# A hybrid encoder block: the recurrence's lowest levels as one block product, and loads, banks and branch tiles rearranged

## The chip, the core and the metric

The kernel runs on one core of one Trainium2 chip. The metric is device microseconds of one execution. Before the change three runs took 1755.15, 1756.07 and 1757.55 us; the median is 1756.07 us. A separate, profiled execution gave the trace.

## The reference

One layer on x of 1024 tokens by 1024 channels, in float32. An RMS norm and one input projection feed three token mixers and three sigmoid gates of 1024 channels:

- a gated linear recurrence (HGRN2): 4 heads, 128 x 128 state, `S_t = diag(f_t) S_{t-1} + (1 - f_t) i_t^T`, `o_t = S_t^T q_t`, then a norm and a silu gate;
- forgetting attention (FoX): 8 heads of 64, causal, with a bias that is the running sum of log-sigmoid forget values;
- attention into 256 memory tokens, 4 heads of 128.

Each mixer's output is projected to 1024 channels, gated and summed; an output projection and the residual follow. Then come a norm, a feed-forward of width 2816 whose gate branch passes a causal convolution of width 3, and the second residual. The recurrence within a chunk needs `A[t,s] = sum_c q[t,c] k[s,c] exp(G[t,c] - G[s,c])` for s <= t, where G is the running sum of log f.

## The kernel before

Products of float32 precision are made from three fast products: an operand is split into a high part (cast on ScalarE, L115) and the rest (VectorE, L123), and `mm3` (L109 to L111) adds high x high, high x low and low x high. Big projections are cut in quarters and done with seven products instead of eight, from sums and differences of the quarters. These operands are "families" (`B11`, `B21`, `T1` to `T4`, `B22`; tiles of pool `pfam`), split once and kept.

The kernel is written as one stream of instructions through a tile framework. The framework orders each engine's queue ahead of time, with its own model of time; an instruction emitted earlier has a higher priority, and `ahead` (L97) raises the priority of a generator's steps by `AHEAD` = 300 instructions. Within a queue the chip then runs in that fixed order. Tiles with a `tag` and `bufs` are rings: a new tile waits until the oldest of the ring is no longer read. A released pool's space is reused tile by tile.

The stages, in order of time:

1. Memory keys and values (`kv_chunk`), squares and turned rows of x, families. The memory's products stay in four PSUM banks, `pairs[0]` and `pairs[2]` (the two `lg` banks); `pairs` are three pairs out of the eight banks, which the next stages take in turn.
2. Five token-major stages (`stage`, 310 us and before): memory queries, HGRN inputs, two of FoX queries and keys, FoX values. `first_unit` does stage 0 with eight plain products, `tm_unit` the others with seven. Results go to DRAM through `put` functions; a part of a `put` that has to turn rows (`queries`, `keys`, tiles `ko` in a ring of two) is put on `pending` and runs one step later. The list `late` says which side work is emitted after which step of a stage. `memory()` (L405: `mem_norm`, `mem_values`, `mem_keys`) is emitted in stage 0 after its third step; `mem_values` copies the values out of the `lg` banks into `mvf`, a tile of the `ko` ring (L317 to L320). Memory attention (`mem_attn`) is cut into 33 steps on the list `slow`, of which `STAGE_STEPS` = 2 are emitted after each stage step; a value step takes two `tr` banks (L669, L674). `forget_row` (L558) computes the running sum of the forget values in two passes of 512 tokens on 8 partitions.
3. FoX, eight heads (`fox_attn`), woven with the channel-major projections (`cm_unit`: 18 units of 7 steps, 12 matmuls of 512 columns a step) that give the recurrence's inputs and the gates. The generator `fill` yields these steps, and `weave` hands out so many per head (`FOX_FILL`). The mask `mskf` is loaded on SP (L908).
4. The recurrence, four heads by two halves of 512 tokens (`hgrn_mix`), woven with the rest of `fill` (`HGRN_FILL`, with `HGRN_STEPS` = 24 for 18 real steps). A half makes `A` in 128-token blocks: the diagonal and its neighbour by one product with `kt` and `qq` (L1022 to L1037), then six levels of block halves, H = 64, 32, 16, 8, 4, 2 (`LEVELS`): differences of G to a reference (L1050, L1051), one exp (L1052), multiplies on GpSimd and VectorE (L1053, L1054), four plain float32 matmuls (L1063, L1072), and a copy under a mask (L1074). Then state and output, the output's norm, and a turned store (L1115 to L1127).
5. The branches (`branches`, L826): the last 48 steps of `fill`, in the order FoX, memory, recurrence. They are in a pool `gp` of their own, which is opened when the projections' ring pool `ur` and `pfam` are released (L898): the mixer's output `yr` (loaded whole, L833 and L835), its split tiles, weights `braw`, gates `gt` and the sums `mg`.
6. The output projection, and the feed-forward up and down, to 1756 us. Only the release of a pool is changed there.

Of the kernel before, what the change touches and what calls it, by code (L numbers as in the profile page):

```python
# [14 lines left out]
P = 128  # L15
# [14 lines left out]
FOX_STEPS, HGRN_STEPS = 28, 24  # L30
# [3 lines left out]
STAGE_STEPS = 2  # L34
# [33 lines left out]
def tile_block(ctx: ExitStack, tc: tile.TileContext, xT, x_rows, memT, mem_rows, vec, fbias, mats, hmask, w_ff, w_tm, w_cm,  # L68
# [247 lines left out]
    def mem_values():  # L316
        mvf = ko_tile("mvf", F32).rearrange("p a b -> p (a b)")  # L317
        for m in range(2):
            S.activation(mvf[:, m * HB:(m + 1) * HB], pairs[2][m], AF.Copy, scale=rm[:, m:m + 1])
        SP.dma_start(kvd[:, 1, :], mvf)  # L320
# [60 lines left out]
    row_norm(1)  # L381

# [21 lines left out]

    def memory():  # L405
        mem_norm()
        mem_values()
        mem_keys()
# [51 lines left out]
    def tm_unit(u, put, between=None):  # L460

        x, z, y = (pairs[(u + i) % 3] for i in range(3))
# [95 lines left out]
    def forget_row():  # L558
        fb = mem["mp"].tile([8, 2], F32, tag="fb", name="fb")
        SP.dma_start(fb[:, 0:1], fbias)  # L560
        for n in range(2):
            sl = slice(n * HB, (n + 1) * HB)
            a, b = (half_tile(f"fr{i}")[:8, :] for i in range(2))
            SP.dma_start(a, ffd[:, sl])
            V.tensor_scalar(a, a, fb[:, 0:1], None, ALU.add)
            S.activation(b, a, AF.Abs)
            S.activation(b, b, AF.Sigmoid)
            S.activation(b, b, AF.Ln)
            V.scalar_tensor_tensor(out=b, in0=a, scalar=0.0, in1=b, op0=ALU.min, op1=ALU.add)
            V.tensor_tensor_scan(a, ones[:8, :].to_broadcast([8, HB]), b, fb[:, 1:2] if n else 0.0,  # L570
                                 ALU.mult, ALU.subtract)
            SP.dma_start(negFd[:, sl], a)
            if n == 0:
                V.tensor_copy(fb[:, 1:2], a[:, HB - 1:HB])
# [64 lines left out]
    def mem_attn(h, n):  # L639
# [26 lines left out]
        def values(j):  # L666
# [7 lines left out]
            po = ps_tr()[:, 0:256]  # L674
# [28 lines left out]
    stage(0, put_mq, (None, second_half, memory, differences, None, third))  # L703
# [10 lines left out]
    for f in pending:  # L714
        f()
    rp.release()
# [104 lines left out]
    pools, mg, y_last = [], [], []  # L821
# [4 lines left out]
    def branches():  # L826
        gp = tc.alloc_tile_pool(name="gp", bufs=1, side="right", reuse_waits="tile")
        pools.append(gp)
        yr = {}

        def load_y(br):
            yr[br] = gp.tile([P, 4, T], F32, tag="y16", name=f"yr{br}")
            SP.dma_start(yr[br][:, 0:2, :], yd3[br][:, 0:2, :])  # L833
            n = 4 if br else 3
            SP.dma_start(yr[br][:, 2:n, :], yd3[br][:, 2:n, :])  # L835

        load_y(ORDER[0])
        ys = [[gp.tile([P, T], F32R, tag=f"y{p}{k}", name=f"y{p}{k}") for p in "hl"] for k in range(4)]
        yh, yl = [a for a, _ in ys], [b for _, b in ys]

        def chunk(br, j):
            raw = gp.tile([P, HB], F32, tag="braw", name="braw", bufs=2)
            SP.dma_start(raw, w_br[br, j])
            wh, wl = (gp.tile([P, HB], F32R, tag=t, name=t, bufs=3) for t in ("bwh", "bwl"))
            split(S, wh, wl, raw)
# [21 lines left out]
        def load_gates(i):  # L867
            gts[i] = []
            for n in range(2):
                gt = gp.tile([P, HB], F32, tag="gt", name="gt", bufs=3)  # L870
# [3 lines left out]
        for i, (br, j) in enumerate(order):  # L874
            if j == 0:
                for c in range(4 if br else 3):
                    split(S, yh[c], yl[c], yr[br][:, c, :])
# [3 lines left out]
                if i < 16:  # L881
                    load_y(order[i + 8][0])
            load_gates(i)
            if i < 8:
                mg.append(gp.tile([P, T], F32, tag=f"mg{j}", name=f"mg{j}"))
# [8 lines left out]

    def fill_steps():
# [757 lines left out]
```

## Time and profile before

| | |
|---|---|
| median of three runs | 1756.07 us |
| the profiled execution, its own time | 1758.42 us |
| its span, first to last instruction | 1756.6 us |
| mean granted TensorE clock | 0.988 |
| busy share of TensorE, VectorE, ScalarE, GpSimd | 97%, 70%, 48%, 25% |
| DMA traffic | 271.96 MB, mean 155 GB/s |

The profile is a page with busy shares and groups of instructions, and a trace that can be asked: who waited for whom, groups by line and shape, one tile's instructions, windows of time, instructions in order of time. A row of a group gives its line, engine, operation, the tiles (written <- read), the shape and the count, then the busy time, the mean duration in ns, and the idle time of the engine ahead of it with what ended it. Matmuls overlap in the pipeline, so the rate of TensorE is read from one start to the next, not from durations. A plain float32 matmul shows as two records.

### The profile page before, as it was taken

How to read it: one execution, taken by the hardware profiler on the slowest of the kernel's cores; microseconds unless marked ns; L12 is line 12 of the kernel's file. 1: busy time of each engine (PE TensorE's matmuls, PEld its weight loads, DVE VectorE, ACT ScalarE, POOL GpSimd, SP SyncE). 2: the span in 40 equal slices, each digit the busy share in tenths (PEclk: the TensorE clock that was granted, in tenths of full speed). 3: DMA queues.
4: the chain of work that ended last, by engine and by line, in shares of the span. 5: the costliest groups of instructions: out<-in, count | busy, mean ns of one | idle time of the engine just before them, and what ended most of it. 6: DMA issues, size and time to landing. Idle time of an engine off the chain costs nothing.

```text
span 1756.6 us, 25190 instructions
## 1 busy us (share of the span) xinstructions
PE 1706.7 (97%) x9040; PEld 1447.6 (82%) x9040; DVE 1228.1 (70%) x2230; ACT 848.2 (48%) x1463; POOL 440.6 (25%) x471
## 2 busy tenths in 40 slices
PE   7899999899999999898999999999999999999999
PEld 5899999778888888787888888788888888788887
DVE  5764665476766666888987845887777877674654
ACT  8655554365655565756432333643343443433332
POOL 0133533454544443443421000211111111100000
PEclk9999999999999999999999999999999999999999
DMA  7252352754444432524443632565444354494772
GB/s 282 92 181 95 133 208 79 206 160 137 145 144 139 138 104 90 179 91 162 164 154 115 209 133 96 157 174 166 149 133 132 114 156 136 151 361 131 242 266 84
DMA packets 119437, 271.96 MB, mean 155 GB/s; under 512 B 12520, under 2 KB 29544, under 8 KB 118672
## 3 DMA queue, kind: packets, MB, share of 16 engines
q1 hardware_dynamic: 95504, 203.76, 34.9%
q0 software_dynamic: 14592, 51.91, 10.4%
q10 hardware_dynamic: 9216, 14.68, 2.3%
q8 instruction: 71, 1.16, 0.3%
q14 instruction: 54, 0.44, 0.1%
HBM read 202.87 MB, written 90.51 MB: 167 GB/s over the span
## 4 chain that ended last, share of the span: by engine, by line
PE 83%; DMA 5%; DVE 4%; ACT 3%; POOL 2%; issue 1%; SPq 1%; ACTq 0%; DVEq 0%; POOLq 0%
PE pp L109 17%; PE pp L110 17%; PE pp L111 17%; PE lg L109 4%; PE lg L110 4%; PE lg L111 4%; PE tr L109 2%; PE tr L110 2%; PE tr L111 2%; PE lg L1072 1%; PE po L981 1%; DMA gd<-uo 1%; PE lg L939 1%; DMA nf<-negFd 1%; PE lg L940 1%
## 5 line engine op out<-in xcount | busy, mean ns | idle before, releaser
L1331 POOL DMA_DIRECT2D rw<-in_w_up x44 | 24.4, 560 | 358.9 <-DVE wl L123 180.6
L115 ACT CAST wh<-s 128x512 fp32r<-128x512 f32 x85 | 51.9, 619 | 127.0 <-PE pp L110 63.5
L115 ACT CAST dwh<-wr 128x1024 fp32r<-128x1024 f32 (+1 forms) x42 | 41.1, 979 | 126.6 <-PE tr L110 42.6
L115 ACT CAST wh<-rw 128x512 fp32r<-128x512 f32 x65 | 40.0, 619 | 87.3 <-PE pp L110 47.6
L1053 POOL TENSOR_TENSOR X<-X,kt 128x256 f32<-128x256 f32 x48 | 52.1, 1090 | 103.0 <-ACT X L1052 101.5
L123 DVE TENSOR_TENSOR dwl<-wr,dwh 128x1024 fp32r<-128x1024 f32 (+1 forms) x42 | 47.6, 1133 | 41.3 <-ACT dwh L115 41.3
L110 PE MATMUL pp<-yl,bwh 128*128 128x512 f32 x192 | 76.3, 397 | 0.0
L123 DVE TENSOR_TENSOR ul<-us,uh 128x512 fp32r<-128x512 f32 x72 | 54.6, 759 | 30.1 <-ACT uh L115 30.0
L109 PE MATMUL pp<-yh,bwh 128*128 128x512 f32 x192 | 75.6, 397 | 0.0
L111 PE MATMUL pp<-yh,bwl 128*128 128x512 f32 x192 | 75.3, 394 | 0.0
L955 ACT ACTIVATE pt<-pt,st 128x128 f32<-128x128 f32 (+3 forms) x64 | 49.7, 777 | 51.6 <-DVE st L952 26.2
L957 POOL TENSOR_SCALAR pt<-pt,st 128x128 f32<-128x128 f32 (+3 forms) x64 | 53.0, 829 | 44.9 <-DVE st L956 32.4
L115 ACT CAST uh<-us 128x512 fp32r<-128x512 f32 x72 | 44.4, 619 | 38.3 <-PE pp L110 27.0
L123 DVE TENSOR_TENSOR wl<-s,wh 128x512 fp32r<-128x512 f32 x85 | 58.2, 685 | 4.9 <-ACT wh L115 4.9
L726 POOL TENSOR_TENSOR us<-ur 128x512 f32<-128x512 f32 x36 | 46.7, 1297 | 44.9 <-DMA ur<-in_w_cm 27.6
L123 DVE TENSOR_TENSOR wl<-rw,wh 128x512 fp32r<-128x512 f32 x65 | 43.8, 687 | 18.9 <-PE pp L111 12.8
L934 POOL TENSOR_TENSOR nfm<-nf,mskf 128x128 f32<-128x128 f32 x64 | 32.9, 515 | 88.5 <-DVE st L945 51.0
L110 PE MATMUL pp<-dbl,dwh 128*128 128x512 f32 x132 | 52.7, 400 | 1.5 <-DVE dbl L123 1.5
L123 DVE TENSOR_TENSOR ul<-ur,uh 128x512 fp32r<-128x512 f32 x54 | 48.3, 896 | 7.8 <-ACT uh L115 6.8
L726 POOL TENSOR_TENSOR us<-us,ur 128x512 f32<-128x512 f32 x36 | 47.6, 1324 | 24.0 <-DVE ul L123 11.5
L123 DVE TENSOR_TENSOR pl<-tr,ph 128x512 fp32r<-128x512 f32 (+1 forms) x80 | 49.6, 629 | 5.9 <-ACT ph L115 5.8
L111 PE MATMUL pp<-dbh,dwl 128*128 128x512 f32 x132 | 53.0, 402 | 0.0
(623 smaller groups left out, 6288.3 us busy)
## 6 DMA issues: line engine op xcount, KB each, us to landing
rw<-in_w_up POOLq DMA_DIRECT2D x44, 512.0 KB, 4.7
ur<-in_w_cm SPq DMA_DIRECT2D x72, 256.0 KB, 2.9
sd<-in_w_dn POOLq DMA_DIRECT2D x30, 512.0 KB, 5.9
br<-yd SPq DMA_DIRECT2D x30, 512.0 KB, 5.5
gd<-uo ACTq DMA_DIRECT2D x48, 256.0 KB, 2.6
gt<-gd SPq DMA_DIRECT2D x48, 256.0 KB, 2.7
yd<-fc SPq DMA_DIRECT2D x44, 256.0 KB, 2.3
raw<-in_w_tm SPq DMA_DIRECT2D x20, 512.0 KB, 4.3
```

The source lines that it names most:

```text
L109: PE.matmul(ps, lh, rh, start=first, stop=False, skip_group_check=more)
L110: PE.matmul(ps, lh, rl, start=False, stop=False, skip_group_check=more)
L111: PE.matmul(ps, ll, rh, start=False, stop=last, skip_group_check=more)
L115: S.copy(out, in_)
L123: return (sub or V).tensor_sub(l, src, h.bitcast(F32))
L726: G.tensor_add(t, a, b)
L934: G.tensor_tensor(nfm, nf[:, tsl], mskf, ALU.add)
L939: PE.matmul(ps[:, :w], qa[:, tsl], kh[:, s0:s0 + w], start=True, stop=False)
L955: S.activation(pt[:, :ns], pt[:, :ns], AF.Exp, bias=st[:, 2:3], accum_out=st[:, 3:4])
L957: G.tensor_scalar(pt[:, :ns], pt[:, :ns], st[:, 3:4], 0.0, ALU.mult, ALU.add)
L1053: G.tensor_mul(Xk, Xk, Kv[:, :, 0, :])
L1331: late["raw"] = G.dma_start(raw[:, 2 * i:2 * i + 2, :], src[:, 2 * i:2 * i + 2, :])
```

## The change

- **Recurrence.** Only levels 64, 32, 16 and 8 remain. The pair product and the levels 4 and 2 are replaced by one product over blocks of eight tokens: with X = G minus G of the block's fourth token, the operands are k exp(-X) and q exp(X), one matmul per 128 tokens, and one copy under a 512-column mask into `A`. `A` is two fixed tiles that are zeroed once. The mask input shrinks from 7 to 4 parts. `HGRN_STEPS` becomes 14.
- **Output of a half.** Norm, turn and store become `finish`, emitted after the next half's block product; its store one half later.
- **Memory.** `mem_norm` and `mem_values` are emitted ahead of stage 0, `mem_keys` in stage 0 after its fifth step; `mvf` moves to the `e` ring (3 tiles). Three slow steps per stage step; a value step reuses the `tr` bank that it turned into. `forget_row` is one pass on 16 partitions, whose second half gets the first half's last sum by a small transfer.
- **Banks.** Stage 4 takes the pairs turned by one.
- **Loads.** The first two steps of `fill` are emitted ahead of the last `pending` work and of FoX; the load of `mskf` gets a priority of 600 instructions.
- **Branches.** No pool of their own: weights in the ring `ur`, gates in the ring `ue`, the outputs `yr` in families `B11` and `B22`, their splits in `B21` and `T2`, the sums in `T1` and `T3`. The first load of `yr` is emitted after the second step of the last projection unit.

The diff, cut to its core:

```
-FOX_STEPS, HGRN_STEPS = 28, 24
+FOX_STEPS, HGRN_STEPS = 28, 14
...
-STAGE_STEPS = 2
+STAGE_STEPS = 3
...
     def mem_values():
-        mvf = ko_tile("mvf", F32).rearrange("p a b -> p (a b)")
+        mvf = e_tile("mvf").rearrange("p a b -> p (a b)")
...
     row_norm(1)
+    mem_norm()
+    mem_values()
...
-        x, z, y = (pairs[(u + i) % 3] for i in range(3))
+        x, z, y = (pairs[(u + i + (u == 4)) % 3] for i in range(3))
...
     def forget_row():
-        fb = mem["mp"].tile([8, 2], F32, tag="fb", name="fb")
-        SP.dma_start(fb[:, 0:1], fbias)
+        fb = mem["mp"].tile([16, 2], F32, tag="fb", name="fb")
+        V.memset(fb, 0.0)
+        a, b = (half_tile(f"fr{i}")[:16, :] for i in range(2))
         for n in range(2):
...
+        V.tensor_tensor_scan(a, ones[:16, :].to_broadcast([16, HB]), b, 0.0, ALU.mult, ALU.subtract)
+        SP.dma_start(fb[8:16, 1:2], a[0:8, HB - 1:HB])
+        V.tensor_scalar(a, a, fb[:, 1:2], None, ALU.add)
...
-            po = ps_tr()[:, 0:256]
+            po = ptr[:, 0:256]
...
-    stage(0, put_mq, (None, second_half, memory, differences, None, third))
+    stage(0, put_mq, (None, second_half, None, differences, mem_keys, third))
...
     stage(4, put_fqk(1))
-    for f in pending:
-        f()
-    rp.release()
...
     def branches():
-        gp = tc.alloc_tile_pool(name="gp", bufs=1, side="right", reuse_waits="tile")
...
+        halves = [[fam_tile(f, p, (P, 2, T)) for f in ("B21", "T2")] for p in "hl"]
+        yh, yl = ([half[k // 2][:, k % 2, :] for k in range(4)] for half in halves)
...
-            raw = gp.tile([P, HB], F32, tag="braw", name="braw", bufs=2)
+            raw = ur.tile([P, HB], F32, tag="ur", name="ur", bufs=5)
...
+    def load_y(br):
+        yr[br] = [fam_tile(("B11", "B22")[ORDER.index(br) % 2], p, (P, 2, T), F32) for p in "hl"]
...
     def fill_steps():
         for u, spec in enumerate(UNITS):
-            yield from cm_unit(u, [puts_of(*s) for s in spec])
+            for i, _ in enumerate(cm_unit(u, [puts_of(*s) for s in spec])):
+                if u == len(UNITS) - 1 and i == 1:
+                    load_y(ORDER[0])
+                yield
+        yield from branches()
         ur.release()
-        pfam.release()
-        yield from branches()
...
     fill = fill_steps()
+    run_all(islice(fill, 2))
+    for f in pending:
+        f()
+    rp.release()
...
-    SP.dma_start(mskf, mats[:, 2 * P:3 * P])
+    with tc.high_priority(2 * AHEAD):
+        SP.dma_start(mskf, mats[:, 2 * P:3 * P])
...
-    LEVELS = [64, 32, 16, 8, 4, 2]
+    LEVELS = [64, 32, 16, 8]
...
+            A = As[n]
+            X, E = (ph.tile([P, HB], F32, tag="X", name=t, bufs=4) for t in "XE")
+            G8 = Gt.rearrange("p (b e) -> p b e", e=8)
+            V.tensor_sub(X.rearrange("p (b e) -> p b e", e=8), G8, G8[:, :, 3:4].to_broadcast([P, HB // 8, 8]))
+            S.activation(E, X, AF.Exp, scale=-1.0)
+            S.activation(X, X, AF.Exp)
+            G.tensor_mul(E, E, kt)
+            V.tensor_mul(X, X, q)
+            pd = ps_lg()
+            for b in range(4):
+                bs = slice(b * P, (b + 1) * P)
+                PE.matmul(pd[:, bs], E[:, bs], X[:, bs], start=True, stop=True)
+            V.copy_predicated(A, hm[:, 2:4, :].rearrange("p a b -> p (a b)"), pd)
             yield
+            for f in range(len(late)):
+                late.pop(0)()
...
+            late.append(partial(finish, h, n, po, gz))
             yield
```

More of the change, by code (lines that the diff above doesn't have):

```diff
@@ L1 @@
 from contextlib import ExitStack, nullcontext
+from functools import partial
 from itertools import chain, islice
@@ L880, in branches @@
                     split(S, yh[3][:, sl], yl[3][:, sl], t)
-                if i < 16:
-                    load_y(order[i + 8][0])
+                if i == 0:
+                    load_y(ORDER[1])
+            if i == 14:
+                load_y(ORDER[2])
             load_gates(i)
             if i < 8:
-                mg.append(gp.tile([P, T], F32, tag=f"mg{j}", name=f"mg{j}"))
+                if j % 2 == 0:
+                    t = fam_tile(("T1", "T3")[j // 4], "hl"[j // 2 % 2], (P, 2, T), F32)
+                    mg.extend(t[:, i, :] for i in range(2))
             for n, ps in chunk(br, j):
@@ L994, in tile_block @@
     ph = tc.alloc_tile_pool(name="ph", bufs=1, side="left", reuse_waits="tile")
[L995 to L996 removed]
+    hm = ph.tile([P, 4, 256], mybir.dt.uint8, tag="hm", name="hm")
+    hmf = ph.tile([P, 4, 64], F32, tag="X", name="hmf", bufs=4)
     rs = ph.tile([P, HB], F32, tag="rs", name="rs")
@@ L1133, in tile_block @@
         weave((ahead(hgrn_mix(h), AHEAD), HGRN_STEPS), (islice(fill, HGRN_FILL[h]), HGRN_FILL[h]))
+    for f in late:
+        f()
     run_all(fill)
```

124 lines of the change are left out of this document (49 added, 75 removed).

## The prediction

> **What bounds the kernel now.** I read the page first, for the busy shares.
>
> ```profile
> span 1756.6 us, 25190 instructions
> ...
> PE 1706.7 (97%) x9040; PEld 1447.6 (82%) x9040; DVE 1228.1 (70%) x2230; ACT 848.2 (48%) x1463; POOL 440.6 (25%) x471
> ```
>
> TensorE is busy all but 50 us, so only two things can shorten the run: matmul time taken away, and idle or slowed TensorE time taken away. The waits of TensorE say what its idle time waited for (total, times, longest).
>
> ```profile
> PE pp L109 <- DVE ko L123: 5.1, 1, 5.1
> PE lg L939 <- DVE st L945: 4.5, 3, 3.8
> ...
> PE lg L1072 <- POOL kt L1019: 3.0, 1, 3.0
> PE tr L1124 <- ACT o L1121: 2.4, 2, 2.2
> ```
>
> Then I cut the span into windows around those waits. The columns are the window, its length, busy time of TensorE, of its weight loads, of VectorE, ScalarE and GpSimd (instructions in brackets), then the granted TensorE clock, the DMA share and GB/s.
>
> ```profile
> 60.00:85.00 25.00, 19.90 (x154) 19.70 (x152) 23.10 (x41) 15.48 (x29) 4.60 (x3) 0.86 0.16 64
> 150.00:175.00 25.00, 22.81 (x180) 22.61 (x180) 12.56 (x20) 15.18 (x26) 6.18 (x8) 0.93 0.27 87
> 300.00:325.00 25.00, 21.60 (x138) 19.46 (x137) 16.16 (x25) 9.58 (x17) 13.82 (x7) 0.86 0.37 134
> 340.00:365.00 25.00, 20.88 (x89) 16.64 (x88) 12.39 (x41) 9.95 (x23) 13.25 (x15) 0.93 0.75 205
> 700.00:760.00 60.00, 54.62 (x278) 45.14 (x278) 48.15 (x85) 39.01 (x62) 26.55 (x24) 0.97 0.45 150
> 815.00:850.00 35.00, 28.74 (x156) 24.55 (x155) 30.57 (x60) 20.57 (x38) 15.74 (x12) 0.85 0.65 233
> 850.00:967.00 117.00, 117.00 (x668) 100.60 (x667) 99.12 (x195) 44.01 (x82) 29.94 (x27) 1.00 0.42 136
> 967.00:1010.00 43.00, 43.00 (x193) 35.57 (x192) 38.47 (x60) 15.86 (x26) 0.00 (x0) 1.00 0.63 213
> ```
>
> The first six windows hold 26.4 us of idle TensorE time, and each also shows a clock below 1: a stretch at half clock follows the wait. Its price is (1 - clock) times the window: 3.5, 1.75, 3.5, 1.75, 1.8 and 5.25 us, 17.5 in all. In matmuls it looks so (start, duration):
>
> ```profile
> 318.34 0.63 PE L110 MATMUL pp<-B11l,uh 128*128 128x512 f32 x1
> 318.76 0.63 PE L111 MATMUL pp<-B11h,ul 128*128 128x512 f32 x1
> ...
> 747.51 0.39 PE L111 MATMUL pp<-T1h,ul 128*128 128x512 f32 x1
> 747.74 0.81 PE L1033 MATMUL lg<-qq,kt 128*128 128x192 f32 x4
> 748.39 1.00 PE L1072 MATMUL lg<-X 128*128 128x64 f32 x8
> ```
>
> The 512-column matmul starts every 0.42 us at half clock and 0.23 us ahead of the next record at full clock. Idle plus clock makes 44 us, an upper end, because a little of the half clock falls inside the idle time.
>
> **The change part by part.** *The block product.* Per half of a head (eight of them) the change drops the two lowest levels and the pair product of diagonal and neighbour, and adds one product over blocks of eight. A plain float32 matmul is two records in the trace. Dropped: 2 levels x 4 matmuls x 2 x 8 = 128 records of 64 columns, and 64 of 192 columns; added: 64 of 128 columns.
>
> ```profile
> 887.24 0.83 PE L1097 MATMUL tr<-hi,kT 128*128 128x128 f32 x6
> 887.91 1.00 PE L1072 MATMUL lg<-X 128*128 128x64 f32 x8
> 888.75 0.38 PE L1033 MATMUL lg<-qq,kt 128*128 128x192 f32 x1
> ```
>
> From start to next start, a 64-column record takes 0.84 / 8 = 0.105 us, a 128-column one 0.67 / 6 = 0.112, a 192-column one (747.74 to 748.39) 0.65 / 4 = 0.163. Removed 128 x 0.105 + 64 x 0.163 = 23.8, added 64 x 0.112 = 7.2: 16.6 us net, and I take **17** because fewer small groups also leave fewer seams between the long matmuls. All of it lies on TensorE's path.
>
> VectorE in the same stage (mean ns after the busy time):
>
> ```profile
> L1054 DVE TENSOR_TENSOR X<-X,hq 128x256 f32<-128x256 f32 x48 | 27.9, 585 | 6.1 <-ACT X L1052 6.0
> L1051 DVE TENSOR_TENSOR X<-Gt 128x256 f32<-128x256 f32 x48 | 24.5, 510 | 0.0
> L1050 DVE TENSOR_TENSOR X<-Gt 128x256 f32<-128x256 f32 x48 | 23.7, 494 | 0.7 <-PE lg L1072 0.3 <-PE lg L1063 0.3
> L1074 DVE COPY_PREDICATED A<-hm,lg 128x256 f32<-128x256 uint8 x32 | 16.5, 515 | 6.6 <-PE lg L1072 6.4
> ...
> L1035 DVE COPY_PREDICATED A<-hm,lg 128x128 f32<-128x128 uint8 x16 | 6.8, 440 | 0.1
> L1034 DVE TENSOR_TENSOR A<-lg,ident 128x256 f32<-128x256 f32 x16 | 6.7, 416 | 1.9 <-PE lg L1033 1.9
> ...
> L1082 DVE TENSOR_TENSOR kE<-Gt 128x512 f32<-128x512 f32 x4 | 2.7, 674 | 0.0
> ```
>
> A half loses 2 x (585 + 510 + 494 + 515) + 2 x (440 + 416) = 5.9 us, and the product of the odd columns (L1025) besides, and gains a subtract and a multiply of 512 columns (0.67 each, the row of the same shape) and a predicated copy of 512 columns, which the trace lacks: between 0.67 and two L1074 rows, 1.03; I take 0.75. Net 3.8 us a half, 30 in all without L1025. On VectorE this shortens nothing directly, since TensorE was full from 850 to 967 with VectorE at 85%; it only lowers the chance of new waits. ScalarE keeps its number of exps. The two GpSimd memsets, and eight mask casts instead of four, run before the first block.
>
> *The five waits.* Six windows, each with what I take of its idle plus clock.
>
> 60:85, at most 8.6 us. TensorE has the next 48 matmuls on the `lg` banks to do, but the banks still hold the memory values:
>
> ```profile
> L319 ACT ACTIVATE mvf<-lg,rm x2: 679/683/687, 79.4 to 79.9; 128x512 f32<-128x512 f32 x2
> ```
>
> The copies out of them ran at 79.4, because `mvf` sat in the ring of two `ko` tiles behind the queries. With `mvf` in the `e` ring and the copies emitted ahead of stage 0, the banks come free before the wait begins. Those 48 matmuls of 256 columns, half a 512 each, are about 5.5 us of cover against 5.1 us of idle time. VectorE, 23.1 of 25 us busy here, stays the late one, so part may come back: I take 6.5. If ScalarE weren't free, the two copies would delay the weights' casts by 1.4 us.
>
> 150:175, at most 3.9. The forget row's two passes become one on 16 partitions, which removes three ScalarE operations and the table loads around them ahead of the exps that TensorE waits for. It adds a small transfer and an add that nobody needs before FoX. But three memory-attention steps per stage step instead of two raise the density right here, and the same chain through GpSimd (L663) stays. I take 2.
>
> 300:325, at most 6.9. Two fill steps (24 matmuls of 0.23, 5.5 us) now stand ahead of the last pending keys; the idle time they cover is 3.4. They need their weights, whose tiles lie where the memory pool was; that pool empties sooner, as one `tr` bank a value step is saved. I take 5.5.
>
> 340:365, at most 5.9. The mask is the last load that FoX needs:
>
> ```profile
> L908 SPq DMA_DIRECT2D mskf<-in_mats x1: 1002/1002/1002, 344.0 to 344.0; - x1
> ```
>
> It was issued at 344.0, behind both heads' loads on SP; the first masked add waited for it, and the logits' banks with it. Doubled priority moves it ahead of those loads and costs them one issue, 1.0 us. I take 5.
>
> 700:760, at most 7.2. The start of the recurrence keeps its shape; only less VectorE and GpSimd work stands in it. I take 3.
>
> 815:850, at most 11.5. Here the branches began: the new pool had to wait for the last projections, `yr` was loaded at 813.7, split from 833, and TensorE had only the recurrence's chain to do.
>
> ```profile
> L833 SPq DMA_DIRECT2D yr<-yd x3: 453/457/496, 813.7 to 913.1; - x3
> ```
>
> With branches in the rings and family tiles, the load starts after the last unit's second product, five products (5 x 2.8 = 14 us) ahead, and the postponed `finish` takes the o chain (L1121) out of the way. What is queued on SP behind the second load, gates and weights of the first chunk, may still be late: I take 8.5.
>
> Sum: 6.5 + 2 + 5.5 + 5 + 3 + 8.5 = 30.5. Against it I set 3.5 us of new waits, about one of the size of 150:175, since the order of every queue is planned anew. Total 17 + 30.5 - 3.5 = 44 us. The profiled execution took 1758.42 us, 1.8 around its span of 1756.6; 44 less is 1714.4. It ran 2.35 above the median of the runs, 1756.07; against that the forecast is **1712**. The lower end, all 44 us of waits and no new one, is 1756 - 61 = 1695.
>
> [...]
>
> **The rivals.** *Waits come back elsewhere.* The matmul time goes, but the planner's new order trades waits for waits, and only the two with a plain cause, the mask and the start of the branches, improve: 17 + 5 + 8.5 - 3.5 = 27, **1729**. For it: every wait above is one instruction late in a fixed order. Against it: four of the six have a named bank, tile or load that the change frees.
>
> *The short waits' half clock stays.* If half clock isn't caused by the short waits, its share in 150:175, 300:325 and 815:850 remains, up to 10.5 us, of which my sum counts about 8: **1720**. Against it: each half-clock stretch in the trace stands right behind a wait. [...]
>
> *The recurrence sets the end of the branches.* The last eight chunks of branches need its last output, and 43 us of matmuls follow that point (window 967:1010).
>
> ```profile
> L1117 ACT ACTIVATE o<-po x8: 579/598/599, 758.8 to 961.0; 128x512 f32<-128x512 f32 x8
> L1052 ACT ACTIVATE X<-X 128x512 f32<-128x512 f32 x48 | 29.9, 634 | 42.3 <-DVE X L1051 38.4 <-PE pp L111 2.8 <-PE po L1103 0.9
> L1053 POOL TENSOR_TENSOR X<-X,kt 128x256 f32<-128x256 f32 x48 | 52.1, 1090 | 103.0 <-ACT X L1052 101.5 <-DMA gd<-uo 1.4
> ```
>
> The halves' squares come every (961.0 - 758.8) / 7 = 28.9 us; the stage from 705 to 1010 is 54 us to the first square, seven such paces, 6 for the last chain, and 43. After the change its TensorE work, without the two early fill steps, is near 305 - 17 - 11.5 - 5.5 = 271, which lets a half take (271 - 54 - 6 - 43) / 7 = 24 us. With 7 steps for 9, the pace would be 22.5 by count; at 27 the stage is 103 + 189 = 292, 13 less than before, and with 19 us from the windows before 700 that is 32: **1724**.
>
> *Slower than before.* The same chain, lengthened. The old pair product needed only `kt` and `qq`; the new one stands behind the running sum, a subtract (0.67), two exps (2 x 0.63) and a GpSimd multiply twice as wide (2 x 1.09), 4.1 us. If the dropped levels ran beside other steps and give the chain nothing back, a half takes 33 us and the stage 103 + 231 = 334: 29 longer, less 19, is 10: **1766**. It decides from 32 us a half on. Against it: the levels already stand behind the same sum, and ScalarE's idle time (38.4 us behind L1051) shows VectorE, which is relieved, as the one that paces them.
>
> **How the numbers follow.** Forecast 0.62 (1696 to 1724 on its own), waits come back 0.18, recurrence at the end 0.10, half clock stays 0.04, slower 0.04, no change 0.02. The range 1696 to 1734 holds the first four, with 5 us on the worst of them. About 0.2% (3.5 us) is what a measurement of this kernel can tell from no change. Faster 0.94, same 0.02, slower 0.04.
>
> **What would show it.** In the changed profile: TensorE's records fall by 128; no wait on `ko` in front of a stage-0 product, none on `st` at the first FoX head, none on `rr` or `o` at the start of the branches; the mask's load lands before the heads' loads; the clock is 1.00 in all windows where a wait is gone; the squares (L1117) come every 24 us or less, and TensorE doesn't idle between the recurrence's last transposes and the last eight chunks. I am wrong if TensorE's idle time in the span is still above 35 us, or if the stage from the first recurrence load to the last branch product isn't at least 20 us shorter.

## The result, and the profile after

The changed kernel took 1727.63 us (median of 4 runs, 1725.94 to 1734.02) beside 1756.81 for the kernel before (median of 4): a ratio of 0.9836 with a 95% interval of 0.9803 to 0.9868, 29 us less. A second batch gave 0.9838 (0.9817 to 0.9860). The forecast was 1712, in a range of 1696 to 1734.

The profiled execution took 1725.94 us, 32.5 less than the profiled one before. Its page, the busy shares:

```profile
span 1724.2 us, 24817 instructions
...
PE 1680.9 (97%) x8912; PEld 1420.8 (82%) x8912; DVE 1204.3 (70%) x2152; ACT 841.7 (49%) x1458; POOL 427.0 (25%) x457
```

TensorE has 128 records fewer, as counted. Its busy time fell by 25.8 us, its idle time only from 49.9 to 43.3. 16.6 of the 25.8 is the matmul time as worked out, and the granted clock is the rest: the trace of before has twelve slots of 3.41 us at half clock (granted 0.50), that of after six, and each costs half of its 3.41 us, 1.7, so 10.2 for six. (The two sum to 1.0 us more than the 25.8; where that went isn't shown.)

The first unit's first product starts at 305.17 us (316.46 before), FoX's last product at 681.73 (699.71), the output projection at 975.62 (1010.13): the stages up to these points got 11.3, 6.7 and 16.5 us shorter, and the rest 2.1 longer. The third stage, the recurrence with the branches, holds all the product's matmul time. Its window, before and after, with columns as in the windows of the prediction:

```profile
699.71:1010.13 310.42, 298.47 (x1614) 252.83 (x1613) 265.75 (x493) 151.82 (x265) 97.95 (x86) 0.98 0.46 152
```

```profile
681.73:975.62 293.89, 281.22 (x1496) 233.99 (x1495) 234.18 (x404) 150.53 (x265) 85.64 (x70) 0.98 0.48 160
```

It gained that time and nothing else: TensorE idles 12.7 us in it, 12.0 before, at the same clock. The windows of the prediction's waits, at their new places in the changed kernel, show where:

```profile
60.00:85.00 25.00, 25.00 (x215) 25.00 (x214) 23.14 (x40) 17.43 (x31) 3.65 (x2) 1.00 0.11 43
150.00:175.00 25.00, 25.00 (x214) 25.00 (x213) 13.70 (x21) 17.07 (x31) 9.77 (x9) 1.00 0.25 86
300.00:325.00 25.00, 24.47 (x135) 20.97 (x135) 17.32 (x25) 12.26 (x21) 13.98 (x7) 1.00 0.50 176
```

```profile
325.00:350.00 25.00, 21.97 (x95) 17.58 (x93) 9.75 (x32) 8.98 (x19) 8.67 (x11) 0.93 1.00 262
682.00:742.00 60.00, 53.71 (x278) 43.61 (x277) 50.13 (x82) 42.14 (x68) 29.10 (x23) 0.97 0.46 153
770.00:818.00 48.00, 41.65 (x225) 33.55 (x224) 38.42 (x72) 30.04 (x54) 22.49 (x16) 0.93 0.47 166
970.00:985.00 15.00, 13.57 (x51) 10.31 (x50) 11.25 (x19) 1.79 (x3) 0.00 (x0) 0.89 0.82 298
```

The first three windows are clean: of 19.4 us (idle plus clock) 0.5 is left. The next three, the starts of FoX, of the recurrence and of the branches, hold 4.8, 8.1 and 9.7 us, 22.6 for 24.6 before. The last, the start of the output projection, lost 3.1 us that it hadn't lost before. The waits behind them, from the list of TensorE's waits after:

```profile
PE pp L111 <- DVE wl L124: 4.0, 5, 2.6
PE lg L1098 <- DVE X L1080: 3.7, 2, 2.3
PE tr L1026 <- ACT o L1023: 3.3, 1, 3.3
...
PE pp L110 <- ACT ue L726: 3.0, 1, 3.0
PE lg L941 <- DMA qa<-kqd: 2.3, 1, 2.3
...
PE pp L111 <- DVE ml L124: 1.3, 1, 1.3
```

Each old name has a new one beside it: at FoX `qa` for `st` (the mask), at the recurrence's start `ue` and X for `ue` and `kt`, at the branches' start still `o`. The 2.6 us on `wl` is the third family's weights at 113.8 us, a new place.

### The profile page after: what moved, and what is told of

It is laid out like the page before. It is cut to its first block, busy times and chain, and to the rows that moved or that the text cites. A ratio compares the mean times of both kernels' runs of the same rounds, so it can differ in the third digit from the quotient of the medians.

```text
span 1724.2 us, 24817 instructions
## 1 busy us (share of the span) xinstructions
PE 1680.9 (97%) x8912; PEld 1420.8 (82%) x8912; DVE 1204.3 (70%) x2152; ACT 841.7 (49%) x1458; POOL 427.0 (25%) x457
## 4 chain that ended last, share of the span: by engine, by line
PE 52%; ACT 1%; DVE 0%; issue 0%; DVEq 0%
PE pp L111 11%; PE pp L110 11%; PE pp L112 11%; PE lg L111 3%; PE lg L110 3%; PE lg L112 3%; PE tr L110 2%; PE tr L111 2%; PE tr L112 2%; PE po L112 1%; PE po L111 1%; PE po L110 1%; PE lg L1098 0%; PE po L1129 0%; PE po L1131 0%; PE tr L1123 0%
## 5 line engine op out<-in xcount | busy, mean ns | idle before, releaser
L116 ACT CAST uh<-ur 128x512 fp32r<-128x512 f32 x78 | 48.0, 616 | 63.5 <-PE pp L111 54.7
L124 DVE TENSOR_TENSOR ul<-ur,uh 128x512 fp32r<-128x512 f32 x78 | 59.8, 767 | 12.3 <-ACT uh L116 11.9
L111 PE MATMUL pp<-B21l,uh 128*128 128x512 f32 x168 | 66.7, 397 | 0.0
L110 PE MATMUL pp<-B21h,uh 128*128 128x512 f32 x168 | 66.5, 396 | 0.0
L110 PE MATMUL pp<-T2h,uh 128*128 128x512 f32 x168 | 66.5, 397 | 0.0
L112 PE MATMUL pp<-T2h,ul 128*128 128x512 f32 x168 | 66.3, 396 | 0.0
L111 PE MATMUL pp<-T2l,uh 128*128 128x512 f32 x168 | 66.3, 395 | 0.0
L112 PE MATMUL pp<-B21h,ul 128*128 128x512 f32 x168 | 66.1, 394 | 0.0
L124 DVE TENSOR_TENSOR wl<-rw,wh 128x512 fp32r<-128x512 f32 x65 | 43.7, 685 | 19.8 <-PE pp L112 15.7
```

The source lines that it names most:

```text
L110: PE.matmul(ps, lh, rh, start=first, stop=False, skip_group_check=more)
L111: PE.matmul(ps, lh, rl, start=False, stop=False, skip_group_check=more)
L112: PE.matmul(ps, ll, rh, start=False, stop=last, skip_group_check=more)
L116: S.copy(out, in_)
L124: return (sub or V).tensor_sub(l, src, h.bitcast(F32))
```

## The experiments

The first theory: the product gives its matmul time wherever it is put, and the shortfall (27 us of waits forecast, about 16 found) lies at the three starts, where the instruction that was late has been relieved and the one behind it on the same path is late instead. Rivals: the product eats part of its own gain, because its exps stand at the head of a half; the postponed `finish`, or the recurrence's pace, makes the new waits. In the batches of the experiments the kernel before took 1759.0 to 1759.3 us (medians). Differences "against the changed kernel" are of the ratios to before, against 0.9838, times 1759.

**The product alone, in the kernel before.**

```
-FOX_STEPS, HGRN_STEPS = 28, 24
+FOX_STEPS, HGRN_STEPS = 28, 19
...
-    LEVELS = [64, 32, 16, 8, 4, 2]
+    LEVELS = [64, 32, 16, 8]
...
+            V.copy_predicated(A, hm[:, 2:4, :].rearrange("p a b -> p (a b)"), pd)
```

> The kernel before with the block product alone (mask, levels, the two kept A tiles; the recurrence's share in the interleave kept by 19 steps for 24, as 14 stands to 18); everything else as before. First theory: the product gives its whole matmul time wherever it is put, 16.6 us by the rows of 64, 128 and 192 columns, and the shortfall of the forecast lies in waits alone: TensorE's records fall by 128, its busy time by 15 to 18 us, and the time by 14 to 20, to 1737 to 1743. Rival: the product's two exps and its subtract now stand at the head of every half, where the old pair product needed only kt and qq, so part of the gain is paid back as new waits at the start of the recurrence: busy time falls by the same 15 to 18, but idle time grows by 4 to 8 and the time falls by 8 to 13 only, to 1744 to 1749.

Measured: 1746.85 us, 0.9931 (0.9919 to 0.9943), 12 us less. Its page, and the rows of a level and of the product (busy, mean ns, idle before):

```profile
span 1742.8 us, 24834 instructions
...
PE 1687.4 (97%) x8912; PEld 1427.0 (82%) x8912; DVE 1205.8 (69%) x2154; ACT 847.9 (49%) x1463; POOL 422.9 (24%) x457
```

```profile
L1065 PE MATMUL lg<-X 128*64 128x64 f32 x128 | 11.3, 234 | 3.4 <-DVE A L1070 3.4
L1038 PE MATMUL lg<-X,E 128*128 128x128 f32 x64 | 9.7, 300 | 4.5 <-DVE X L1034 4.5
```

The rival holds here: busy time fell by 19.3 us, idle time grew by 5.5 (55.4 for 49.9), and the product itself waited 4.5 us for its operand from VectorE.

**The old product, in the changed kernel.**

```
-FOX_STEPS, HGRN_STEPS = 28, 14
+FOX_STEPS, HGRN_STEPS = 28, 18
...
-    LEVELS = [64, 32, 16, 8]
+    LEVELS = [64, 32, 16, 8, 4, 2]
...
+                V.tensor_mul(A3[:, 2 * d:2 * d + 2, :], pd[:, :, 0:P], ident.unsqueeze(1).to_broadcast([P, 2, P]))
```

> The changed kernel with the old pair product and the six levels put back (18 steps in the interleave, the true count, as 14 is after); the queues, tiles and postponed finish stay. First theory: it loses the product's matmul time and nothing else: 16 to 19 us slower than the changed kernel, 1744 to 1747, and the waits of 700 to 737 us stay near 6 us idle. Rival, that the product's exps at the head of a half cause the waits at the recurrence's start: idle time there falls to 3 us or less, and it is only 10 to 14 us slower, 1738 to 1742.

Measured: 1747.01 us, 0.9927 (0.9912 to 0.9941): 15.7 us slower than the changed kernel. On top of the other edits the product gives nearly its full time, as the first theory says. The profile's idle time is 42.0 us in all (1740.5 less 1698.5 busy), the changed kernel's 43.3; at the recurrence's start it is 4.0, between the two expectations:

```profile
700.00:760.00 60.00, 55.96 (x310) 46.72 (x310) 56.10 (x102) 42.19 (x70) 34.78 (x27) 0.97 0.31 103
```
Seen from the other side, everything but the product is worth 12.8 us (10 to 15), where the prediction had 27.

The equal sums of idle time hide an exchange. With the old product the start of the branches is nearly clean (770:835 loses 2.3 us, where 770:818 of the changed kernel loses 9.7), and the end of the recurrence is late instead: 880:1010 idles 6.1 us and has two slots at half clock, and 3.2 us of that is a wait for the last `o` at 957 us. The changed kernel idles only 1.4 us from 860 to 995.

**finish at once, and the recurrence's pace.**

```
-            late.append(partial(finish, h, n, po, gz))
+            finish(h, n, po, gz)
```

> The changed kernel with finish called at once, at the end of its own half, instead of behind the next half's block product; its store at once too. First theory: the postponement keeps the o chain out of TensorE's way, and without it two or three waits on o come back: 3 to 8 us slower than the changed kernel, 1731 to 1736. Rival: the postponement moved the o chain onto the splits of y at the start of the branches and made the 3.3 us wait on o there; without it that wait and its half clock go: 2 to 5 us faster, 1723 to 1726.

```
-FOX_STEPS, HGRN_STEPS = 28, 14
+FOX_STEPS, HGRN_STEPS = 28, 19
```

> The changed kernel with 19 recurrence steps counted in the interleave for the true 14, the ratio of the kernel before (24 counted for 18): a head's recurrence is emitted in the first three quarters of its fill. First theory: the waits at the recurrence's start come from too much ScalarE and VectorE work at once, and emitting the steps closer together makes them longer: 2 to 6 us slower than the changed kernel, 1730 to 1734. Rival: the recurrence's pace decides nothing, since the fill covers it: within 2 us of the changed kernel, and waits of the same sum at other places.

Measured: 1729.08 us, 0.9823 (0.9810 to 0.9837), and 1730.84 us, 0.9830 (0.9815 to 0.9845): neither differs from the changed kernel by what can be told. In both a wait on `o`, of 4.9 and 4.8 us, stands at the start of the branches. The postponement neither makes that wait nor prevents it; both expectations for it fail, and for the pace its rival holds.

**The first unit's stores on ScalarE's queue.** In the changed kernel's timeline SP stands at a store of `hgd` until VectorE has its tile, and behind it stand the mask and FoX's loads:

```profile
322.26 0.53 SPq L620 DMA_DIRECT2D kqd<-ko  x1
325.16 0.33 SPq L766 DMA_DIRECT2D hgd<-uo  x1
325.54 0.43 SPq L910 DMA_DIRECT2D mskf<-in_mats  x1
...
328.19 0.75 SPq L917 DMA_DIRECT2D qa<-kqd  x1
```

```
-            SP.dma_start(dst, t)
+            (S if h == 0 and what < 2 else SP).dma_start(dst, t)
```

> The changed kernel with the first unit's four stores to hgd issued from ScalarE's queue instead of SP's, where the loads of FoX's first head stand behind them (one of them waited there from 322.8 to 325.2 us). First theory: the 2.3 us wait of the first logits on qa is this place in SP's order; the loads start 2 us earlier, the wait falls below 0.7 us and the half clock behind it goes: 2 to 4 us faster than the changed kernel, which stands at 0.9836 of the kernel before, so 0.9813 to 0.9825. Rival: the keys' own writes and the transfers set it (the DMA queues move 320 to 410 GB/s there), so the loads land when they did: within 1 us, the wait at 1.5 us or more.

Measured: 1725.90 us, 0.9812 (0.9796 to 0.9828), 4.6 us less than the changed kernel, with intervals that overlap (0.9817 to 0.9860 there). The same stretch of its timeline and its window:

```profile
322.17 0.52 SPq L620 DMA_DIRECT2D kqd<-ko  x1
322.74 0.63 SPq L910 DMA_DIRECT2D mskf<-in_mats  x1
```

```profile
325.00:350.00 25.00, 24.06 (x113) 19.70 (x113) 13.11 (x40) 12.22 (x26) 12.29 (x13) 1.00 1.05 277
```

The mask is issued 2.8 us earlier and the loads behind it 1.3 to 2.6 us, TensorE idles 0.9 us in the window instead of 3.0, and the half clock is gone: 3.8 us at this place. The first theory holds, in the profile more surely than in the time (the wait on `qa` is 0.9, above the 0.7 expected).

**The mask at plain priority.**

```
-    with tc.high_priority(2 * AHEAD):
+    if True:
```

> The changed kernel with the mask's load at plain priority, behind both heads' loads on SP, as in the kernel before. First theory: the doubled priority of the mask is worth little, because the load of qa is what is late there now; with the plain one the mask comes 9 us later and is late again: the wait at the start of FoX grows from 2.3 to 4 us or more, and the time by 1 to 3 us, 0.983 to 0.985 of before. Rival: the prediction's term, 5 us: 0.986 or more. Second rival: nothing, since the earlier start of FoX hides it: within 1 us.

Measured: 1729.98 us, 0.9834 (0.9816 to 0.9852), the changed kernel's time.

```profile
L910 SPq DMA_DIRECT2D mskf<-in_mats x1: 348/348/348, 341.6 to 341.6; - x1
```

```profile
325.00:350.00 25.00, 21.13 (x84) 16.80 (x83) 6.80 (x10) 6.32 (x11) 4.99 (x5) 0.86 1.01 242
770.00:818.00 48.00, 46.68 (x273) 39.12 (x272) 44.62 (x82) 32.42 (x58) 19.82 (x19) 1.00 0.58 197
```

The mask is issued 16 us later than after, and the start of FoX loses 7.4 us of idle and clock for 4.8. So the priority is worth 2.6 us at the start of FoX; the loads are late with or without it (here 2.3 us on `qa` and 1.6 on `kl`). But behind the start, from 350 us to FoX's last product, TensorE idles 5.3 us here for 1.0, 4.3 of it in short waits on `st`. Whether the late mask or the new order of the queues makes these isn't shown, so over FoX as a whole the priority may be worth 2.6 us or up to 6.9, and the 5 of the prediction is not refuted. In the total it is gone: the branches' start loses 1.3 us here for 9.7. For the time the second rival holds; what the loads do at the start of FoX is as the first theory has it.

**The product behind the levels.**

```
             A = As[n]
...
+            for li, H in enumerate(LEVELS):
+                if li == 1:
+                    for f in range(len(late)):
+                        late.pop(0)()
...
+            V.copy_predicated(A, hm[:, 2:4, :].rearrange("p a b -> p (a b)"), pd)
+            yield
```

> The changed kernel with the block product emitted behind a half's four levels instead of ahead of them (finish of the half before goes behind the first level). First theory: the product's subtract, two exps and 512-column multiplies at the head of a half are what makes the start of the recurrence late (idle 6.3 us from 700 to 737); behind the levels they have cover: idle there at most 3 us, and 3 to 6 us faster than the changed kernel, 0.980 to 0.982 of before. Rival: whatever stands first at the head of a half waits for the same running sum, table loads and full VectorE, and the product behind is then what the output product waits for: within 2 us, idle there still 5 us or more, or moved to the end of a half.

Measured: 1719.62 us, 0.9780 (0.9758 to 0.9802), 10 us less than the changed kernel.

```profile
700.00:740.00 40.00, 35.41 (x189) 28.50 (x189) 33.13 (x57) 28.18 (x47) 23.33 (x18) 0.91 0.29 96
...
770.00:811.00 41.00, 37.84 (x223) 31.67 (x221) 38.12 (x68) 29.96 (x54) 15.58 (x15) 1.00 0.60 215
```

The gain is larger than expected and not where it was expected. From 700 to 740 TensorE still idles 4.6 us, and with the clock it loses 8.2 there, the changed kernel's 700 to 740 7.9. The branches' start loses 3.2 for 9.7. The first theory's reason falls with its place; the wait at the recurrence's head stays. There, in the changed kernel, ScalarE has this to do before the copy that frees TensorE's bank:

```profile
698.57 1.28 ACT L1043 ACT_TABLE_LOAD   x1
699.87 0.72 ACT L1043 ACTIVATE L<-ha,c 128x512 f32<-128x512 f32 x1
700.61 1.28 ACT L1053 ACT_TABLE_LOAD   x1
...
703.47 0.57 ACT L726 COPY ue<-pp 128x512 f32<-128x512 f32 x1
```

Two table loads around one logarithm, 3.3 us, stand ahead of the copy, and behind them two exps and a cast, 1.6 us. With the product behind the levels the order is nearly the same, and the wait for the copy is 3.1 us. Taking the logarithm out of there wasn't tried, so that the table loads make the wait is argued from the order alone.

**What happens at the branches' start.** GpSimd's timeline in the changed kernel, then VectorE's beside it:

```profile
797.44 7.55 POOL L1047 TENSOR_SCALAR kt<-ha,c 128x512 f32<-128x512 f32 x1 [1.97 <-DVE rr L128]
804.96 1.62 POOL L129 TENSOR_TENSOR rr<-rr,mhalf 128x4 f32<-128x4 f32 x1
```

```profile
797.66 2.34 DVE L124 TENSOR_TENSOR B21l<-B11h,B21h 128x1024 fp32r<-128x1024 f32 x2
...
801.47 2.35 DVE L124 TENSOR_TENSOR T2l<-B11l,T2h 128x1024 fp32r<-128x1024 f32 x2
...
804.35 0.68 DVE L136 SCALAR_TENSOR_TENSOR uo<-pp,ue 128x512 f32<-128x512 f32 x1
```

The multiply `kt`, usually 0.70 us, took 7.55. VectorE ran without a pause meanwhile, and `kt` ended at 804.99 us, 0.64 us after the product with `pp` (L136) began. Behind it stood the power of `finish` (L129), and behind that the scaling of `o`, TensorE's 3.3 us wait. The profiles of the other runs fit: in the six with a `kt` of 7.54 or 7.55 us (the changed kernel twice, `finish` at once, the pace, the first stores, the spread splits) a wait on `o` of 3.3 to 4.9 us stands at the branches' start, and in the five in which no `kt` took more than 3.07 us (the product behind the levels, with and without the stores, the plain mask, and the first and third of the following) none does. Three experiments on it. The first leaves out the scaling of the recurrence's output by its own norm:

```
-            S.activation(o2[:, b, :], po[:, b * P:(b + 1) * P], AF.Copy, scale=rr[:, b:b + 1])
+            S.activation(o2[:, b, :], po[:, b * P:(b + 1) * P], AF.Copy, scale=mhalf[:, b:b + 1])
```

> The changed kernel with the recurrence's output scaled by a constant column instead of its own inverse root mean square (this part of the norm is left out; the sum and the power are still computed, but nobody waits for them). First theory: the 3.3 us wait on o at 803 us is GpSimd's power, queued behind a multiply that GpSimd stretched to 7.6 us because VectorE, with the splits of y back to back, left it no gap; without that link the wait and the half clock behind it go: 3 to 6 us faster than the changed kernel, 0.980 to 0.982 of before. Rival: TensorE is short of work there because VectorE itself is full, and the next thing that VectorE owes is late instead: within 2 us, another wait of 2 us or more between 790 and 815 us.

Measured: 1724.09 us, 0.9799 (0.9782 to 0.9815), 6.9 us less than the changed kernel. No wait on `o` is left, and the window loses 1.4 us for 9.7. But the edit did more than cut the link: the order of GpSimd's queue changed too, `kt` runs at 792.7 us, ahead of the splits, and takes 0.80. So this run doesn't tell the link from the long multiply.

```profile
770.00:818.00 48.00, 46.63 (x270) 38.59 (x270) 44.07 (x82) 33.23 (x61) 19.34 (x17) 1.00 0.62 221
```

Next, the splits of y spread over the last unit, and no longer ahead of the first chunk:

```
+                if u == len(UNITS) - 1 and 2 <= i < 6:
+                    split_y(ORDER[0], i - 2)
```

> The changed kernel with the four splits of the first branch's y emitted one by one behind the third to sixth product of the last unit, instead of all four ahead of the first chunk. First theory: spread out they leave GpSimd gaps, its multiply takes 2 us or less, and the wait on o falls below 1.5 us: 2 to 5 us faster than the changed kernel, 0.981 to 0.983 of before. Rival: VectorE has 4.8 us of splits to do beside a recurrence that keeps it full from 770 to 805 us, wherever they stand, so a wait of 2 us or more stays in 770 to 815: within 2 us.

Measured: 1729.01 us, 0.9826 (0.9806 to 0.9845), no difference, and it decides nothing: the splits stayed at the same place in VectorE's queue, and `kt` as it was.

```profile
799.12 7.54 POOL L1055 TENSOR_SCALAR kt<-ha,c 128x512 f32<-128x512 f32 x1 [1.97 <-DVE rr L128]
```

So the third takes the low parts off VectorE; ScalarE writes a second cast in their place, so the low parts of the first branch's y are left out:

```
-                    split(S, yh[c], yl[c], yr[br][c // 2][:, c % 2, :])
+                    split(S, yh[c], yl[c], yr[br][c // 2][:, c % 2, :]) if i else [S.copy(t[c], yr[br][c // 2][:, c % 2, :]) for t in (yh, yl)]
```

> The changed kernel with the low parts of the first branch's y written by ScalarE (a second cast of the same source, so that the first branch's low parts are wrong) instead of VectorE's four subtracts of 1024 columns. First theory: GpSimd's multiply at the start of the branches took 7.6 us because those subtracts left it no gap between VectorE's instructions; without them it takes 2 us or less, the wait on o falls below 1.5 us, and the kernel is 3 to 6 us faster than the changed one, 0.980 to 0.982 of before. Rival: the recurrence's own work fills VectorE there; the multiply stays above 4 us, the wait on o at 2.5 us or more, and the time within 2 us.

Measured: 1724.78 us, 0.9814 (0.9794 to 0.9833), 4.2 us less, with overlapping intervals.

```profile
797.02 3.07 POOL L1047 TENSOR_SCALAR kt<-ha,c 128x512 f32<-128x512 f32 x1 [5.04 <-DVE rr L128]
800.06 1.01 POOL L129 TENSOR_TENSOR rr<-rr,mhalf 128x4 f32<-128x4 f32 x1
```

```profile
799.11 0.41 DVE L1077 TENSOR_TENSOR X<-Gt 128x256 f32<-128x256 f32 x1
```

`kt` falls from 7.55 to 3.07, ending 0.6 us after VectorE paused at 799.5, and the wait on `o` is gone. Without the low parts `kt` is 4.5 us shorter, so they are most of the cause; that what it still has above the usual 0.70, 2.4 us, is VectorE's other work is the author's estimate. The place gains less than the wait: 770:818 still loses 7.3 us, for 9.7, because two slots run at half clock, now behind waits of 1.0 us on X and 1.4 on `ue`, a copy of ScalarE's, which has four casts more to do there:

```profile
770.00:818.00 48.00, 44.02 (x255) 36.07 (x254) 38.26 (x79) 36.10 (x63) 20.18 (x19) 0.93 0.54 186
```

With the product behind the levels `kt` has its usual length, and that kernel, too, has no wait on `o`:

```profile
803.30 0.69 POOL L1047 TENSOR_SCALAR kt<-ha,c 128x512 f32<-128x512 f32 x1 [3.44 <-DVE kE L1111]
```

**The changed kernel again, and two edits together.**

> The changed kernel once more, unaltered, beside the others of this batch, since its first interval (0.9803 to 0.9868) is wider than the differences in question. Both theories: a ratio between 0.981 and 0.985, 1726 to 1732 beside a kernel before of 1759.

Measured: 1731.38 us, 0.9838 (0.9817 to 0.9860), as expected. Its profile has a span of 1728.7, 4.5 above the first one's, with a 4.9 us wait on `o` for 3.3: single waits of one kernel differ by this much between executions.

```
-            SP.dma_start(dst, t)
+            (S if h == 0 and what < 2 else SP).dma_start(dst, t)
...
+            for li, H in enumerate(LEVELS):
+                if li == 1:
...
+            V.copy_predicated(A, hm[:, 2:4, :].rearrange("p a b -> p (a b)"), pd)
```

> The changed kernel with the two experiments that went ahead of it put together: the block product behind the levels (0.978 of before) and the first unit's stores from ScalarE's queue (0.9812). First theory: they mend waits at different places, 331 us and 770 to 815 us, and add up: 2 to 3 us faster than the product behind the levels alone, 0.976 to 0.977. Rival: the order of every queue behind the first edit is planned anew, and what one gains is lost at another place: 0.978 to 0.980.

Measured: 1718.48 us, 0.9775 (0.9758 to 0.9792), 11 us less than the changed kernel and faster than both kernels, but not to be told from the product behind the levels alone. Whether the two edits add up stays open: the wait of 2.2 us on `qa` is gone and TensorE's first logits wait 1.2 us for nothing that the profile shows, while the logits' waits on `st` took 2.5 us (0.4 without the stores' edit).

## Why the prediction was right, and where it was wrong

**The matmul time: right.** 17 us was forecast, by the distance from start to start of 64-, 128- and 192-column records; the 0.4 us of it above 16.6, for fewer seams, is shown by no run. The product brought 15.7 on top of the other edits; alone, 17.6 without the idle time that it added (12.1 and 5.5). Only the slower rival had seen that the product's operands come through a longer chain; alone, that is what it waited for, and 5.5 us is far from the 29 that the rival would have needed. VectorE's relief was 28.7 us in the recurrence's own lines (164.9 to 136.2 us of durations), for the 30 forecast, and 23.8 on the page.

**The first three waits: right, and too low.** 6.5 + 2 + 5.5 = 14.0 was taken; the windows gave 19.4 - 0.5 = 18.9, the half clock included. Each had one named bank or tile, and work enough behind it: with `mvf` copied early TensorE went straight on through the 48 matmuls on `lg`, and nothing came back in that window; whether the new waits on the weights at 101 to 117 us are the same lateness moved isn't shown. Nor does a run take one of these three edits back by itself: that each did its part is read from the windows, and the experiments give only the sum of everything but the product, 12.8 us.

**The last three waits: this is the step that failed.** 5 + 3 + 8.5 = 16.5 was taken; the windows gave 24.6 - 22.6 = 2.0. "The mask is the last load that FoX needs" was true by little: with the mask early `qa` and `kl` are late, on the same queue, and SP's own wait at a store sets them (the stores' queue alone was worth 3.8 us at this place); the mask's priority was worth 2.6 us there. With the mask at plain priority 4.3 us more of idle time stand in the rest of FoX, so the size of that term stays open. At the recurrence's start I counted VectorE and GpSimd and wrote "ScalarE keeps its number of exps"; of the waits that are left the longest, 3.0 us, is for ScalarE's copy of `ue`, behind a logarithm with two table loads that no edit touches, and 2.3 us are for X from VectorE. That the table loads hold the copy is not shown, so the cause stays open here. At the branches' start "the postponed `finish` takes the o chain (L1121) out of the way" was wrong: the wait on `o` comes with and without it. The earlier `yr` put y's splits, back to back on VectorE, beside the recurrence, and beside them a multiply of GpSimd's took 7.55 us (3.07 without their low parts, 0.70 usually), on a 25% busy engine that I had looked at only for its sums.

**The new waits: half.** 3.5 us was set aside; the weights at 101 to 117 us took 3.5 and the output projection's first products 3.1. Why `ml` is late there wasn't tried. In the sum: 16.6 + 18.9 + 2.0 - 6.6, and 1.7 for a half clock behind the 1.5 us wait on `dbl` that didn't come again, is 32.6, the profiled 32.5.

**The rivals.** "Waits come back elsewhere" gave 1729 and the time is 1728, but it named the mask and the branches' start as the two that would improve, and they are two of the three that hardly did (1.1 and 1.8 us by the windows): a right number by a wrong sum. The forecast's own theory was good for 1696 to 1724; that 1728 lies in the stated range is owed to the width taken from this rival, not to the sum. "The short waits' half clock stays" fell: with the waits of 150:175 and 300:325 their half clock went. The recurrence's squares come every (926.7 - 737.9) / 7 = 27.0 us, the pace that the third rival needed for 1724, yet TensorE is busy without a break from 816 us to the end of that stage: here the pace decided nothing. With the old product it did, by the 3.2 us wait for the last `o`.

```profile
L1019 ACT ACTIVATE o<-po x8: 577/598/604, 737.9 to 926.7; 128x512 f32<-128x512 f32 x8
```

**The tests set beforehand.** Records, `ko`, `st`, the mask's order and the clock in the first three windows came as said; the wait on `o`, the pace of 24 us, TensorE's idle time (43.3, limit 35) and the recurrence's stage (from its first load, at 701.4 us before and 684.0 after, 17.1 us shorter, 20 asked) did not. Two of these were named as proof of being wrong, and rightly: they are the same failed step.

## What to carry to other kernels

Take the whole of a wait as a gain only when its one late instruction is named and there is work enough behind it; where a stage starts, look for the second-latest operand on the same path, on queues and engines that the edit doesn't touch. A little-used GpSimd in a chain was a risk here: beside a VectorE without a gap its multiply of 0.70 us took 7.55. And a small edit of the order moved waits at places far from it (with the mask at plain priority the branches' start lost 1.3 us for 9.7), so read its worth at its own place and in the time, and trust it only where both agree.

## What the runs showed of the chip

**Half clock came in stretches of 3.41 us.** In the traces of the kernel before and of the changed one the stretches at a granted clock of 0.50 lasted 3.41 us (six before, six after) or 6.83 us (three before), but for one that begins 1.1 us ahead of the end of the changed kernel's span. Within each trace their starts lie on one grid: 207 steps of 3.413 us from 36.54 to 743.10 us before, 205 from 36.92 to 736.65 after. The length of a wait alone did not decide whether such a stretch followed. Two slots of the changed kernel around the wait on `qa`, then two around the longer wait on `wl`, then two of the kernel with the plain mask around the same `wl`, there 2.2 us long:

```profile
330.47:333.88 3.41, 1.35 (x6) 0.78 (x5) 0.86 (x2) 0.62 (x1) 2.48 (x2) 1.00 1.04 244
333.88:337.29 3.41, 3.17 (x9) 2.62 (x10) 0.53 (x1) 0.00 (x0) 0.00 (x0) 0.50 1.06 280
```

```profile
111.99:115.40 3.41, 1.80 (x16) 1.60 (x14) 0.44 (x3) 0.68 (x3) 0.00 (x0) 1.00 0.98 330
115.40:118.82 3.42, 2.40 (x20) 2.40 (x21) 2.08 (x5) 0.71 (x2) 0.00 (x0) 1.00 1.07 307
```

```profile
113.67:117.08 3.41, 1.31 (x11) 1.31 (x12) 2.29 (x6) 0.49 (x2) 0.00 (x0) 1.00 1.11 280
117.08:120.49 3.41, 3.41 (x19) 3.41 (x18) 1.38 (x2) 1.17 (x2) 0.00 (x0) 0.50 1.02 379
```

A slot with 1.31 or 1.35 us of TensorE work was followed by one at half clock. The 2.6 us wait on `wl`, cut by a slot's edge so that the two slots have 1.80 and 2.40 us of work, was followed by full clock (TensorE's next half clock is at 333.9 us). Busy time alone does not tell the slots apart, though: in the changed kernel slots with 1.82, 1.93 and 1.98 us (from 733.24, 794.68 and 975.59) were followed by half clock, one with 1.63 (from 1077.98) by full clock, and what else counts isn't shown. So the waits of 2.2 and 2.3 us were each followed by a slot that cost 1.7 us more, the one of 2.6 us by none. Part of the spread between runs of one kernel may be this: of the changed kernel's first four runs the fastest, 1725.94 us, had a mean clock of 0.994, the slowest, 1734.02, one of 0.988.

**One GpSimd multiply took 0.69 to 7.55 us.** `kt`, of one shape, took 7.55 us in the changed kernel, where VectorE ran without a pause beside it, 3.07 with the low parts on ScalarE, and 0.69 with the product behind the levels. The first ended 0.64 us after VectorE's product with `pp` began, the second 0.6 us after VectorE paused. That VectorE's work made it long is shown by the second alone; which of its instructions hold GpSimd, and by what, isn't shown, and the record of the long `kt` begins at 797.44 us, 0.2 ahead of the splits.
